# Every 4th or 8th chunk of split weights placed 32, 64 or 96 bytes further in its buffer

## The chip, the cores and the metric

The kernel runs on one core of a Trainium2 chip. The metric is device time in microseconds (us) of one execution. TensorE (PE in the profile) multiplies; its weight loads have a row of their own (PEld). VectorE is DVE, ScalarE is ACT, GpSimd is POOL, and SyncE (SP) starts most transfers. SBUF is the memory on the chip from which all of them read; a buffer's address here means its byte offset within a partition.

## The reference

Two transformer blocks follow each other on one sequence of 256 tokens of width 1024, in float32. Cut to what matters:

```
# first block
proj = rms_norm(x) @ w_in;  x = x + [attention, gated linear attention] @ w_out
h = causal_dwconv(rms_norm(x) @ w_ffn_up)          # 1024 -> 2 x 2816
x = x + (silu(h_gate) * h_val) @ w_ffn_down        # 2816 -> 1024
x = rms_norm(x)
# second block
x = x + 0.5 * g1 * swiglu(h1, ffn1_w_in_2, ffn1_w_out_2)   # 1024 -> 2 x 2816 -> 1024
z = h2 @ w_in_2;  y_a = latent attention @ w_branch_a;  y_b = chunk attention @ w_branch_b
x = x + g2 * ((sigmoid(gate_a) * y_a + sigmoid(gate_b) * y_b) @ w_out_2)
x = x + 0.5 * g3 * swiglu(h3, ffn2_w_in_2, ffn2_w_out_2)
return rms_norm(x)
```

h1, h2 and h3 are normalised x, scaled and shifted by vectors that come from w_ada_2.

## The kernel before

Activations lie feature-major: a tile has 128 features on the partitions and the 256 tokens along the row. A linear layer (`lin_t`) makes 128 output features at a time: it goes over the 128-row blocks k of the weight matrix and adds up in one PSUM bank.

Float32 accuracy is reached with three matmuls for each block. The weights w are split into a rounded part and a rest, w = wh + wl, the activations likewise into xh + xl, and wh·xh, wh·xl and wl·xh are added up. Each of the three loads its own 128x128 weights (a LDWEIGHTS) and streams 256 columns of activations; in the layers that read an unnormalised x it is 258 columns, where the two more carry a shift vector. `lin_r`, used in a few places, swaps the two: activations are the loaded side and 512 columns of weights are streamed.

All weights come from HBM as one stream, packed in the order of their use into 285 chunks of up to 128x1024 (the list `PLAN`, made by `plan`). The class `Stream` handles them: `load` starts a chunk's transfer into a buffer `wraw`; `prep` makes two tiles, `whi` and `wlo`, each from a ring of 4 buffers (`SPLIT_BUFS`), and lets ACT write the rounded part into `whi`; `low` lets DVE write the rest (`wraw` - `whi`) into `wlo`; `next` hands out the blocks of a chunk, normally 8 blocks of 128 columns, so 24 matmuls for a chunk. Eight chunks (`UNCUT`) are not split and are used as plain float32. All instructions are recorded through a helper, so every row of the profile has the line L453; tiles tell them apart: `nh`, `nl` are the halves of a normalised input, `hh`, `hl` those of a feed-forward's hidden layer, `xhi`, `xlo` those of an unnormalised x.

The order in which side work is put between the matmuls is made at build time by a model of the engines' clocks; addresses have no part in it.

In the program before, every `whi` and `wlo` buffer is 4096 bytes long and starts at 64 modulo 128 (for example 78016, 82112, 86208, 90304 for `whi`), and every block of activations that such weights meet starts at 0 modulo 128. A block of weights is 512 bytes of a row, so each load starts at 64 modulo 128 too.

Of the kernel before, what the change touches and what calls it, by code (L numbers as in the profile page):

```python
# [11 lines left out]
F32R = mybir.dt.float32r  # L12
# [6 lines left out]
P = 128  # L19
# [5 lines left out]
CH = 1024  # L25
# [152 lines left out]

LINE = 32
XROW = 9 * LINE  # L180
SKIP = {"const": 0, "y1": 0, "hid1": 0, "ff1": 0, "y2": 0, "att2c": 16, "mgc": 0, "ff2": 0}
RAW_PAIRS = {'w_ffn_up': 2, 'ffn1_w_in_2': 5, 'ffn2_w_in_2': 5}
PLAN, UNCUT = plan()
# [27 lines left out]
class Stream:  # L211
# [20 lines left out]
    def prep(self, upto):  # L232
        while self.n_prep <= min(upto, len(PLAN) - 1):
            c = self.n_prep
            w = CW[c]
            self.load(c)
            raw = self.raw.pop(c)
            self.n_prep += 1
            if c in UNCUT:
                self.ready[c] = (raw, raw)  # L240
                continue
            hi = self.pool.tile([P, CH], F32R, name="whi", bufs=SPLIT_BUFS)
            lo = self.pool.tile([P, CH], F32R, name="wlo", bufs=SPLIT_BUFS)
            self.act.activation(hi[:, :w], raw[:, :w], AF.Copy)
            self.ready[c] = (hi, lo)
            self.owed[c] = (raw, self.clock.t["act"])
# [54 lines left out]
def rows(pool, k, w, name, skip=0, dtype=F32R, **kw):  # L301

    t = pool.tile([P, LINE + k * w if skip else k * w], dtype, name=name, **kw)
    return t[:, skip:skip + k * w].rearrange("p (k w) -> p k w", k=k)


def parts(pool, k, name, skip=0, w=S):

    a, b = (rows(pool, k, w, n, skip) for n in name)
    return Operand(a, b, k)  # L310
# [236 lines left out]
SPLIT_BUFS = 4  # L547
# [3 lines left out]
def block_kernel(ctx: ExitStack, tc: tile.TileContext, xin, wst, adaw, cin, vec, cst_a, cst_b, cst_l, wgu, pos,  # L551
# [161 lines left out]
    def xop():  # L713

        return parts(const, KD, ("xhi", "xlo"), SKIP["const"], XROW)

# [154 lines left out]
    actx = ExitStack()  # L871
    xo = parts(const, KD, ("xhi", "xlo"), SKIP["const"])
    xo.f = rows(ypool, KD, S, "yh", SKIP["y1"], F32)
    ap = actx.enter_context(tc.tile_pool(name="att1", bufs=2))
# [90 lines left out]

    yo = parts(ypool, KD, ("yh", "yl"), SKIP["y1"])
    am = {}
# [167 lines left out]
    for what, n in steps(MIX1):  # L1135
# [23 lines left out]
        else:  # L1159
# [3 lines left out]
            state[what] = True  # L1163
    xo = Operand(None, None, KD, f=rows(const, KD, S, "xg", SKIP["const"], F32, tag="xhi"))
    ss = SumSq("ssa")
# [61 lines left out]
    fp = fctx.enter_context(tc.tile_pool(name="ffn1p", bufs=2))  # L1227
    ho = parts(hpool, NF, ("hh", "hl"), SKIP["hid1"])
    no = parts(hpool, KD, ("nh", "nl"), SKIP["hid1"])
# [607 lines left out]
```

## Time and profile before

| | us |
|---|---|
| median of 3 executions | 886.78 |
| the three executions | 882.56, 886.85, 886.78 |
| the profiled execution | 880.52 |
| its span, first to last instruction | 878.7 |
| PE busy | 865.8 (99%) |
| PEld busy | 835.2 (95%) |
| DVE busy | 699.0 (80%) |
| ACT busy | 501.4 (57%) |

PE is busy when any matmul is under way; since matmuls overlap in the records (each shows 0.28 us, and one starts about every 0.12 us), 99% does not say that they follow each other as closely as they could. Time outside the span is 1.8 us. The granted clock is full (1.00) up to the last microseconds.

### The profile page before, as it was taken

Reading aid. Unit: us, or ns where it says so; the run is one execution under the profiler, and the core shown is the slowest. Engines: PE = TensorE matmul, PEld = TensorE weight load, DVE = VectorE, ACT = ScalarE, POOL = GpSimd, SP = SyncE. Lnnn points to the kernel's source line nnn. Section 1 sums busy time; section 2 is a strip of 40 time slices with the busy share of each in tenths; the row PEclk is TensorE's granted clock in tenths of the full one; section 3 lists DMA queues with packets and bytes.
Section 4 is the critical chain, followed back from the end, with each engine's and each line's share of the span. In section 5 each row is a group of like instructions: output and inputs, shape, how many; then the busy total and the mean of one; then the engine's idle time right before and its main releaser. Section 6 shows DMA issues by size and latency. Waiting matters only on the chain.

```text
span 878.7 us, 18127 instructions
## 1 busy us (share of the span) xinstructions
PE 865.8 (99%) x7290; PEld 835.2 (95%) x7290; DVE 699.0 (80%) x1289; ACT 501.4 (57%) x858; POOL 39.5 (4%) x78
## 2 busy tenths in 40 slices
PE   9999999999999999999999999999999999999996
PEld 7878898999999999999999998999999999999996
DVE  5869677999998889989987789889889985555553
ACT  5846676666665557544554466565646754445441
POOL 0000000000000000010110000000000000000000
PEclk9999999999999999999999999999999999999998
DMA  8534344777777985688898755776777675665541
GB/s 313 185 116 140 120 145 151 261 234 234 229 234 269 305 289 171 234 314 282 313 336 275 258 193 181 258 262 208 232 227 238 193 222 186 189 192 168 192 145 48
DMA packets 54132, 192.05 MB, mean 219 GB/s; under 512 B 6016, under 2 KB 6528, under 8 KB 54048
## 3 DMA queue, kind: packets, MB, share of 16 engines
q1 hardware_dynamic: 42768, 151.28, 51.4%
q0 software_dynamic: 10560, 38.41, 13.7%
q8 instruction: 57, 0.93, 0.4%
q10 hardware_dynamic: 720, 1.21, 0.4%
q14 instruction: 27, 0.22, 0.1%
HBM read 189.82 MB, written 1.05 MB: 217 GB/s over the span
## 4 chain that ended last, share of the span: by engine, by line
PE 95%; DVE 3%; DMA 1%; ACT 1%; issue 0%; DVEq 0%; SPq 0%; ACTq 0%
PE acc L453 89%; PE sca L453 3%; PE sct L453 2%; PE ob L453 1%; DVE wlo L453 1%; DMA wraw<-in_wst_dram 1%; DVE ad L453 0%; DVE x L453 0%; DVE f L453 0%; DVE kf L453 0%; DVE sm L453 0%; DVE kcat L453 0%; DVE m L453 0%; ACT rsqt L453 0%; ACT whi L453 0%
## 5 line engine op out<-in xcount | busy, mean ns | idle before, releaser
L453 DVE TENSOR_TENSOR wlo<-wraw,whi 128x1024 fp32r<-128x1024 f32 (+1 forms) x277 | 333.5, 1211 | 65.8 <-ACT whi L453 65.2
L453 ACT ACTIVATE whi<-wraw 128x1024 fp32r<-128x1024 f32 (+1 forms) x277 | 285.6, 1043 | 47.8 <-issue 30.0
L453 PE MATMUL acc<-nh,whi 128*128 128x256 f32 x1048 | 294.5, 281 | 0.0
L453 PE MATMUL acc<-nl,whi 128*128 128x256 f32 x1048 | 291.9, 279 | 0.0
L453 PE MATMUL acc<-nh,wlo 128*128 128x256 f32 x1048 | 291.5, 278 | 0.0
L453 PEld LDWEIGHTS acc<-nh,whi 128*128 128x128 f32 x1048 | 196.8, 188 | 2.3 <-issue 2.2
L453 PEld LDWEIGHTS acc<-nl,whi 128*128 128x128 f32 x1048 | 196.5, 188 | 0.1
L453 PEld LDWEIGHTS acc<-nh,wlo 128*128 128x128 f32 x1048 | 196.6, 188 | 0.0
L453 PE MATMUL acc<-hh,whi 128*128 128x256 f32 x528 | 147.0, 278 | 0.0
L453 PE MATMUL acc<-hl,whi 128*128 128x256 f32 x528 | 147.0, 278 | 0.0
L453 PE MATMUL acc<-hh,wlo 128*128 128x256 f32 x528 | 146.8, 278 | 0.0
L453 PEld LDWEIGHTS acc<-hh,whi 128*128 128x128 f32 x528 | 99.2, 188 | 0.0
L453 PEld LDWEIGHTS acc<-hh,wlo 128*128 128x128 f32 x528 | 99.0, 188 | 0.0
L453 PEld LDWEIGHTS acc<-hl,whi 128*128 128x128 f32 x528 | 99.0, 187 | 0.0
L453 DVE SCALAR_TENSOR_TENSOR adraw<-adraw,crow 128x1024 f32<-128x1024 f32 x72 | 87.7, 1218 | 6.3 <-DMA adraw<-in_adaw_dram 6.2
L453 PE MATMUL acc<-xhi,whi 128*128 128x258 f32 (+2 forms) x312 | 90.9, 291 | 0.7 <-DVE x L453 0.7
L453 PE MATMUL acc<-xlo,whi 128*128 128x258 f32 (+2 forms) x312 | 87.9, 282 | 0.0
L453 PE MATMUL acc<-xhi,wlo 128*128 128x258 f32 (+2 forms) x312 | 87.6, 281 | 0.0
L453 POOL DMA_DIRECT2D adraw<-in_adaw_dram x72 | 38.1, 529 | 641.5 <-DVE adraw L453 374.7
L453 PEld LDWEIGHTS acc<-xhi,whi 128*128 128x128 f32 (+1 forms) x312 | 58.5, 188 | 3.0 <-issue 2.3
L453 PEld LDWEIGHTS acc<-xlo,whi 128*128 128x128 f32 (+1 forms) x312 | 58.7, 188 | 0.4
L453 PEld LDWEIGHTS acc<-xhi,wlo 128*128 128x128 f32 (+1 forms) x312 | 58.5, 188 | 0.0
(283 smaller groups left out, 1151.2 us busy)
## 6 DMA issues: line engine op xcount, KB each, us to landing
wraw<-in_wst_dram SPq DMA_DIRECT2D x277, 512.0 KB, 4.4
adraw<-in_adaw_dram POOLq DMA_DIRECT2D x72, 512.0 KB, 5.0
wraw<-in_wst_dram SPq DMA_DIRECT2D x7, 256.0 KB, 3.2
rb<-in_rel_dram SPq DMA_DIRECT2D x4, 384.0 KB, 4.4
f<-in_cst_l_dram SPq DMA_DIRECT2D x1, 576.0 KB, 6.4
x<-in_xin_dram SPq DMA_DIRECT2D x2, 256.0 KB, 6.1
x<-in_xin_dram ACTq DMA_DIRECT2D x2, 256.0 KB, 6.6
crow<-in_cin_dram POOLq DMA_DIRECT2D x1, 512.0 KB, 7.6
```

What stands on the lines that cost most here:

```text
L453: return f(*args, **kw)
```

## The change

The buffers `whi` and `wlo` grow by 32 floats (128 bytes), and a chunk's tile is a view of 1024 floats inside. For most chunks the view starts at 0. For a chunk whose number in `PLAN` is divisible by `every` it starts 8, 16 or 24 floats (32, 64 or 96 bytes) in, by a table that gives `every`, the start in `whi` and the start in `wlo` for each matrix.

```
+APART = {"w_ffn_up": (4, 8, 8), "w_ffn_down": (8, 8, 8), "ffn1_w_in_2": (4, 0, 8), "ffn1_w_out_2": (4, 24, 24),
+         "ffn2_w_in_2": (4, 16, 16), "ffn2_w_out_2": (4, 8, 0)}
...
-            hi = self.pool.tile([P, CH], F32R, name="whi", bufs=SPLIT_BUFS)
-            lo = self.pool.tile([P, CH], F32R, name="wlo", bufs=SPLIT_BUFS)
+            every, *apart = APART.get(PLAN[c][0][0], (4, 8, 8))
+            hi, lo = (self.pool.tile([P, CH + LINE], F32R, name=n, bufs=SPLIT_BUFS)[:, a:a + CH]
+                      for n, a in zip(("whi", "wlo"), (0, 0) if c % every else apart))
```

Matrices that the table leaves out have (4, 8, 8). 68 of the 277 split chunks are moved:

| matrix | chunks split | of them moved | whi, wlo by bytes |
|---|---|---|---|
| w_in, w_out | 30 | 8 | 32, 32 |
| w_ffn_up | 40 | 10 | 32, 32 |
| w_ffn_down | 22 | 3 | 32, 32 |
| ffn1_w_in_2 | 44 | 11 | 0, 32 |
| ffn1_w_out_2 | 22 | 6 | 96, 96 |
| w_in_2 to w_out_2 | 53 | 13 | 32, 32 |
| ffn2_w_in_2 | 44 | 11 | 64, 64 |
| ffn2_w_out_2 | 22 | 6 | 32, 0 |

The built program has the same instructions in the same order on every engine, with the same waits. Only addresses differ: the buffers of both rings now lie 4224 bytes apart, those behind them (work tiles, hidden layers) 1024 bytes further up. Modulo 128 nothing moves but the chunks of the table, from 64 to 96, 0 or 32.

## Rows read from the trace of the kernel before

**Rows 1.** The page: busy time by engine, and the chain that ended last.

```profile
PE 865.8 (99%) x7290; PEld 835.2 (95%) x7290; DVE 699.0 (80%) x1289; ACT 501.4 (57%) x858; POOL 39.5 (4%) x78
...
PE 95%; DVE 3%; DMA 1%; ACT 1%; issue 0%; DVEq 0%; SPq 0%; ACTq 0%
PE acc L453 89%; PE sca L453 3%; PE sct L453 2%; PE ob L453 1%; DVE wlo L453 1%; DMA wraw<-in_wst_dram 1%; DVE ad L453 0%; DVE x L453 0%; DVE f L453 0%; DVE kf L453 0%; DVE sm L453 0%; DVE kcat L453 0%; DVE m L453 0%; ACT rsqt L453 0%; ACT whi L453 0%
```

**Rows 2.** The chain in order of time: start, length, work (longest pieces).

```profile
138.44 189.79 PE acc L453 x1566
...
329.09 178.31 PE acc L453 x1560
...
686.37 183.56 PE acc L453 x1554
```

**Rows 3.** Windows in the feed-forwards, 256-column matmuls: first block, ff1, ff2.

```profile
core 0: us, PE busy (x) PEld busy (x) DVE busy (x) ACT busy (x) POOL busy (x), PEclk, DMA share, GB/s
149.50:323.50 174.00, 174.00 (x1477) 173.95 (x1476) 160.26 (x264) 108.40 (x172) 11.10 (x21) 1.00 0.78 252
355.00:506.50 151.50, 151.50 (x1339) 151.50 (x1338) 130.47 (x208) 75.70 (x109) 15.34 (x29) 1.00 0.84 290
711.50:868.00 156.50, 156.50 (x1332) 156.50 (x1331) 87.28 (x110) 73.50 (x104) 0.00 (x0) 1.00 0.54 171
```

**Rows 4.** Timeline of PE at 500 us, in ff1: start and length in us.

```profile
499.74 0.28 PE L453 MATMUL acc<-hh,whi 128*128 128x256 f32 x1
499.86 0.28 PE L453 MATMUL acc<-hl,whi 128*128 128x256 f32 x1
...
500.99 0.28 PE L453 MATMUL acc<-hh,wlo 128*128 128x256 f32 x1
```

**Rows 5.** Timeline of PE at 800 us, in ff2.

```profile
799.79 0.28 PE L453 MATMUL acc<-nh,whi 128*128 128x256 f32 x1
...
801.09 0.28 PE L453 MATMUL acc<-nh,wlo 128*128 128x256 f32 x1
```

**Rows 6.** Windows with no other PE work, outside the feed-forwards.

```profile
115.50:134.00 18.50, 18.50 (x158) 18.45 (x157) 14.15 (x24) 12.44 (x24) 0.00 (x0) 1.00 0.52 172
628.50:653.00 24.50, 24.50 (x213) 24.33 (x212) 20.55 (x37) 11.68 (x18) 1.58 (x3) 1.00 0.79 258
660.00:681.00 21.00, 21.00 (x181) 21.00 (x180) 20.00 (x36) 13.11 (x23) 1.59 (x3) 1.00 0.74 236
```

**Rows 7.** Windows of 258-column matmuls, before ff1's and ff2's stretches.

```profile
330.00:354.00 24.00, 24.00 (x202) 24.00 (x201) 23.62 (x50) 17.50 (x30) 0.53 (x1) 1.00 0.52 177
684.00:710.00 26.00, 26.00 (x217) 25.95 (x216) 24.54 (x47) 18.50 (x29) 0.00 (x0) 1.00 0.59 189
```

**Rows 8.** Timeline of PE where ff1 goes from 258 to 256 columns.

```profile
353.57 0.29 PE L453 MATMUL acc<-xlo,whi 128*128 128x258 f32 x1
353.70 0.28 PE L453 MATMUL acc<-xhi,wlo 128*128 128x258 f32 x1
353.82 0.29 PE L453 MATMUL acc<-xhi,whi 128*128 128x258 f32 x1
...
354.90 0.28 PE L453 MATMUL acc<-nh,whi 128*128 128x256 f32 x1
355.02 0.28 PE L453 MATMUL acc<-nl,whi 128*128 128x256 f32 x1
355.13 0.28 PE L453 MATMUL acc<-nh,wlo 128*128 128x256 f32 x1
```

**Rows 9.** The page's costliest groups: PE's three kinds of inputs, and the split.

```profile
L453 DVE TENSOR_TENSOR wlo<-wraw,whi 128x1024 fp32r<-128x1024 f32 (+1 forms) x277 | 333.5, 1211 | 65.8 <-ACT whi L453 65.2
L453 ACT ACTIVATE whi<-wraw 128x1024 fp32r<-128x1024 f32 (+1 forms) x277 | 285.6, 1043 | 47.8 <-issue 30.0
L453 PE MATMUL acc<-nh,whi 128*128 128x256 f32 x1048 | 294.5, 281 | 0.0
...
L453 PE MATMUL acc<-hh,whi 128*128 128x256 f32 x528 | 147.0, 278 | 0.0
```

## The prediction

> **What bounds the kernel now.** I read the page first: PE is on the chain for 95% of the span, and DVE, the next busiest, for 3% [rows 1]. The chain in order of time then shows that this is no mixture: three pieces of 190, 178 and 184 us, one for each feed-forward, hold nothing but matmuls into `acc` [rows 2], 552 of 879 us. In there no wait can be shortened. What counts is only how soon one matmul follows the other.
>
> That is read from windows laid inside these pieces. In the first block's feed-forward 1477 matmuls stand in 174.0 us, 117.8 ns each; in ff2 1332 in 156.5 us, 117.5 ns; in ff1 1339 in 151.5 us, 113.1 ns [rows 3]. The matmuls are of one shape, and PE is busy for the whole of each window, so PE waits for nobody in any of them. The timeline says the same: 11 steps take 1.25 us at 500 us [rows 4] and 1.30 us at 800 us [rows 5], 113.6 against 118.2 ns. So one and the same program text runs at two paces that lie 4.5 ns apart, about 113.3 (fast) and 117.8 (slow).
>
> What makes the difference? Not the clock, granted in full (1.00) in all three windows. Not transfers: the fast window has the busiest DMA, 0.84 against 0.78 and 0.54. Not DVE or ACT: ff2's window has the least of both per us and is slow. Not the addresses as such, since ff1 and ff2 lay out the same buffers and the weights start at 64 and the activations at 0 modulo 128 in both. And no pace gives way to the other inside a window. It looks like a relation in time between two streams, the load of the next weights and the columns of the running matmul, that is settled when a stretch begins and then repeats itself. In ff1 one sees it settle: the steps of the 258-column matmuls are uneven (0.13 and 0.12 us), and with the third 256-column matmul the steps are down to 0.11 us [rows 8]. Both streams read SBUF, so an address can enter such a relation. That is the lever which this change has; the trace does not show it pulled.
>
> The executions fit this. Against the profiled 880.52 the median is 6.3 us longer, and 1339 matmuls of ff1 at 4.5 ns more are 6.0 us. So I take it, as an estimate, that the usual execution is slow in ff1 too.
>
> **The change part by part.** *Instructions:* none is added, removed or moved, and no wait changes. So nothing new queues behind anything, on any engine or queue, SP's and POOL's included.
>
> *The split on ACT and DVE:* 277 activations of 1043 ns and as many subtractions of 1211 ns [rows 9] write as many bytes as before. I cost it at nothing. The cover is room on DVE: 160 of 174 us in the tightest window [rows 3]. A tenth more on 68 moved chunks would be 68 x 0.12 = 8 us of DVE spread over the kernel, against 14 us idle in that one window, so it would still be hidden.
>
> *The moved chunks themselves:* the trace has no weights at 96, 0 or 32 modulo 128, so the pace in them is bounded. From below by the fast pace, the lowest of any 256-column row. From above by the least regular rows I have, the 258-column matmuls: 24.0 us for 202 and 26.0 us for 217, 118.8 to 119.8 ns on the mean [rows 7], with single steps of 0.13 us [rows 8]. I take 117.8, the slow pace, which lies between and is nearest to these means. Where the stretch was slow before, that costs nothing. In ff1, fast in the profiled execution, 208 matmuls read a moved operand (64 in the way in, where 8 of the moved chunks meet 256 columns and only `wlo` moves; 6 x 24 in the way out), and they lose 208 x 4.5 ns = 0.9 us.
>
> *The chunks after a moved one:* here is the whole gain or loss. Entering and leaving a moved chunk changes the relation between the two streams in mid-run, every 96 matmuls (every 192 in `w_ffn_down`). The relation may settle anew each time, in the slow pace or in the fast one; without the change it never gets a second chance. Bounds for this: all unmoved chunks slow, ff1 included (+6.0 us on the profiled execution), and all of them fast. For the second: of the 1477 matmuls of the first feed-forward's window 13 x 24 = 312 read a moved operand, 1165 do not, and 1165 x 4.5 ns = 5.2 us. In ff2's window 288 do (8 chunks of 24, and 6 chunks in which only `whi` moves, 16 each), 1044 do not: 4.7 us. The stretches outside, 158 + 213 + 181 = 552 matmuls [rows 6] at 116 to 117 ns with windows' edges counted in, keep three quarters unmoved: 414 x 4.5 = 1.9 us. In attention, short matmuls break the stream every few microseconds; there I count nothing.
>
> I take the upper bound for the unmoved chunks: a relation that has its neighbour 4.5 ns away and gets a kick of 32, 64 or 96 bytes some 60 times has many chances to fall into the better one, and the better one, once there, held for 1339 matmuls [rows 3].
>
> *Sum:* 880.5 - 5.2 - 4.7 - 1.9 + 0.9 = 869.6, so 870 us. Every term is an absolute pace, so this end does not depend on which of its executions the kernel before was caught in; against the median of 886.8 it is 1.9% less.
>
> The Trainium skill speaks against all of it. In "SBUF — State Buffer", section "Who interferes with whom", TensorE has two read ports in SBUF, one for the moving operand and one for LDWEIGHTS, independent of each other, and "PE and ACT never wait on anyone". By that no address can change a matmul's pace, and the sum would be the 886.8 of before. The trace agrees only in part: nobody else's traffic moves the pace [rows 3], but something that is not the shape, the clock or another engine does, by 4.5 ns. So I give the rule a rival's chance and not more.
>
> **The rivals.**
>
> *The kick takes in one place only.* If of the two slow feed-forwards only one turns fast, the sum is 880.5 - 5.2 + 0.9 = 876. With ff1 slow and the others fast it is 869.6 + 5.1 = 875. For it: three matrices of different table entries must each fall right. Against it: the same relation, modulo 128, holds in all of them. 874 to 882.
>
> *Nothing happens.* The pace does not hang on the address, or each stretch falls back into the pace it would have had: between 880.5 and 886.8 by the share of fast stretches, and 887 if the usual execution is the slow one throughout. For it: within 174 us of slow pace [rows 3] side work on DVE, ACT and DMA comes and goes and never knocks the relation loose, so it may not be easily moved. 882 to 891.
>
> *Slower: moved chunks run at the pace of the uneven rows, and what follows stays slow.* Some 1310 matmuls read a moved operand (68 chunks of up to 24, less the halves that stay). All of ff1 slow is +6.0 us. At 119.8 ns, the mean of the 258-column row, moved matmuls cost 2.0 ns over the slow pace: 880.5 + 6.0 + 2.6 = 889. At 125 ns, a single step of the uneven kind throughout, they cost 7.2 ns: 880.5 + 6.0 + 9.4 = 896. It decides from 3.6 ns over the slow pace, about 121.4 ns in moved chunks. Against it: no 20 us of this trace run that slowly.
>
> **How the numbers follow.** Kick works in nearly all stretches (862 to 874): 0.44. In one place only (874 to 882): 0.20. Nothing (882 to 891): 0.22. Slower (over 891): 0.14. The lower end: the two feed-forward inputs of the page have 3 x (1048 + 528) = 4728 matmuls [rows 9], with the 552 outside 5280; less the 1339 already fast, 3941 x 4.5 = 17.7 us, and 880.5 - 17.7 = 863 with moved chunks fast as well. The likeliest case alone spans 863 to 874. For 8 in 10 I leave out the slower rival and the top of the third: 863 to 889. Half a per cent is 4.4 us, about what a measurement of this kernel can tell from no change; so faster means under 882.3: 0.44 + 0.20 = 0.64, same 0.22, slower 0.14.
>
> **What would show it.** Right: windows in the first feed-forward and ff2 with about 88 matmuls for each 10 us instead of 85, moved chunks at about 118 ns between chunks at 113; the same counts of instructions; DVE's 1211 ns and ACT's 1043 ns unchanged. Wrong in the step on moved chunks: a pace above 120 ns in every fourth chunk of a timeline. Wrong in the step on what follows: unmoved chunks still at 117.8 in the first feed-forward and ff2, or ff1 fallen to it. Wrong altogether: the two paces as before, in other stretches than before.

## The result and the profile after

The changed kernel takes 873.47 us (median of 4 executions, 873.32 to 873.88), the kernel before 886.75 (882.56 to 886.85): a ratio of 0.985, interval 0.984 to 0.987. The forecast was 870, faster. So the number held; what made it is another matter, as the experiments show. In the comparisons of the experiments the kernel before ran near 881 us about as often as near 887 (17 and 20 of 39 executions), so the gain is 7 to 13 us, by which of the two one meets.

The chain in order of time of the changed kernel, its longest pieces (start, length, work), against [rows 2]:

```profile
138.39 184.33 PE acc L457 x1566
323.58 180.07 PE acc L457 x1560
...
680.57 182.37 PE acc L457 x1554
```

The first block's feed-forward gave 189.79 - 184.33 = 5.5 us, ff2 1.2 us, and ff1, the fast one of before, lost 1.8. The spans differ by 878.7 - 871.8 = 6.9 us, so 2.0 us came from outside the three pieces.

Windows of the changed kernel inside these pieces, then outside them, then in 258-column matmuls, against [rows 3, 6, 7]. A window also counts the two or three matmuls that hang over its edges:

```profile
core 0: us, PE busy (x) PEld busy (x) DVE busy (x) ACT busy (x) POOL busy (x), PEclk, DMA share, GB/s
149.50:318.50 169.00, 169.00 (x1481) 168.95 (x1480) 158.39 (x266) 108.60 (x172) 11.09 (x21) 1.00 0.80 261
349.00:502.00 153.00, 153.00 (x1336) 153.00 (x1335) 131.59 (x208) 76.77 (x110) 15.32 (x29) 1.00 0.83 286
707.00:861.00 154.00, 154.00 (x1321) 154.00 (x1320) 86.02 (x107) 72.24 (x103) 0.00 (x0) 1.00 0.54 171
115.50:134.00 18.50, 18.50 (x160) 18.40 (x159) 13.97 (x24) 12.76 (x24) 0.00 (x0) 1.00 0.51 171
624.50:649.00 24.50, 24.50 (x216) 24.33 (x213) 20.81 (x39) 12.12 (x18) 1.59 (x3) 1.00 0.82 264
655.00:676.00 21.00, 21.00 (x186) 21.00 (x185) 20.46 (x39) 13.57 (x23) 1.67 (x4) 1.00 0.77 251
325.00:348.00 23.00, 23.00 (x194) 23.00 (x193) 22.71 (x48) 16.94 (x27) 0.53 (x1) 1.00 0.55 185
679.00:704.00 25.00, 25.00 (x208) 24.95 (x207) 23.50 (x45) 17.71 (x28) 0.00 (x0) 1.00 0.58 185
```

These are 114.1, 114.5 and 116.6 ns per matmul in the three feed-forwards, means of more than one pace; the granted clock is 1.00 in all windows. Outside, they are 115.6, 113.4 and 112.9 where they were 117.1, 115.0 and 116.0, so most of these stretches turned fast too; the 258-column matmuls stayed at 118.6 and 120.2 where they were at 118.8 and 119.8. The timeline takes the feed-forwards apart: the chunks are counted off in it, 24 matmuls each, back from the first matmul that reads `hh`. In the first block's feed-forward these five rows are the first matmuls of five chunks in a row; the first chunk is a moved one:

```profile
221.21 0.28 PE L457 MATMUL acc<-nh,whi 128*128 128x256 f32 x1
...
224.00 0.28 PE L457 MATMUL acc<-nh,whi 128*128 128x256 f32 x1
...
226.72 0.28 PE L457 MATMUL acc<-nh,whi 128*128 128x256 f32 x1
...
229.44 0.28 PE L457 MATMUL acc<-nh,whi 128*128 128x256 f32 x1
...
232.16 0.28 PE L457 MATMUL acc<-nh,whi 128*128 128x256 f32 x1
```

2.79 us for the moved chunk (about 116.5 ns each), then 2.72 us three times (113.3). The same five places in ff2, again beginning with a moved chunk:

```profile
747.67 0.28 PE L457 MATMUL acc<-nh,whi 128*128 128x256 f32 x1
...
750.54 0.28 PE L457 MATMUL acc<-nh,whi 128*128 128x256 f32 x1
...
753.38 0.28 PE L457 MATMUL acc<-nh,whi 128*128 128x256 f32 x1
...
756.20 0.28 PE L457 MATMUL acc<-nh,whi 128*128 128x256 f32 x1
...
758.92 0.28 PE L457 MATMUL acc<-nh,whi 128*128 128x256 f32 x1
```

2.87 us (about 119.9 ns each) for the moved chunk, 2.84 and 2.82 us (117.9, slow), then 2.72 (113.3, fast). This pattern repeats in every round of four, and in ff2's way out with 117.6 ns in the moved chunk. The important row is the fourth: the time per matmul falls at a chunk that is not moved, behind another that is not moved. In the trace of the kernel before no stretch changes its pace between chunks. Something else than the moved chunks can turn a stretch fast, and the only other thing that the diff changes is that buffers lie 4224 bytes apart instead of 4096. 4224 is 16 times 256 plus 128: modulo 128 all stays as it was, but modulo 256 the unmoved chunks now start at 64 and 192 in turn, where all started at 192 before.

The work on ACT and DVE cost what it did [rows 9]:

```profile
L457 DVE TENSOR_TENSOR wlo<-wraw,whi 128x1024 fp32r<-128x1024 f32 (+1 forms) x277 | 333.5, 1211 | 65.3 <-ACT whi L457 64.4
L457 ACT ACTIVATE whi<-wraw 128x1024 fp32r<-128x1024 f32 (+1 forms) x277 | 285.7, 1044 | 44.6 <-issue 30.3
```

### The profile page after: what moved, and what is told of

Same layout as the page of the kernel before. It is cut to its first block, busy times and chain, and to the rows that moved or that the text cites. A ratio compares the mean times of both kernels' runs of the same rounds, so it can differ in the third digit from the quotient of the medians.

```text
span 871.8 us, 18127 instructions
## 1 busy us (share of the span) xinstructions
PE 857.0 (98%) x7290; PEld 827.0 (95%) x7290; DVE 698.3 (80%) x1289; ACT 502.2 (58%) x858; POOL 39.4 (5%) x78
## 4 chain that ended last, share of the span: by engine, by line
PE 95%; DVE 3%; DMA 1%; ACT 0%; issue 0%; SPq 0%; DVEq 0%; ACTq 0%
PE acc L457 89%; PE sca L457 3%; PE sct L457 2%; DMA wraw<-in_wst_dram 1%; PE ob L457 1%; DVE wlo L457 1%; DVE ad L457 0%; DVE x L457 0%; DVE kf L457 0%; DVE f L457 0%; DVE sm L457 0%; DVE kcat L457 0%; ACT rsqt L457 0%; SPq L457 0%; DVE am L457 0%
## 5 line engine op out<-in xcount | busy, mean ns | idle before, releaser
L457 DVE TENSOR_TENSOR wlo<-wraw,whi 128x1024 fp32r<-128x1024 f32 (+1 forms) x277 | 333.5, 1211 | 65.3 <-ACT whi L457 64.4
L457 ACT ACTIVATE whi<-wraw 128x1024 fp32r<-128x1024 f32 (+1 forms) x277 | 285.7, 1044 | 44.6 <-issue 30.3
```

What stands on the lines that cost most here:

```text
L457: return f(*args, **kw)
```

## The experiments

All kernels have the same instructions in the same order with the same waits; they differ only in where `whi` and `wlo` lie. What lies behind these buffers moves by multiples of 256 bytes, so no run moves an activation modulo 256. Where a cut of code shows added lines alone, they stand in place of the three lines of the change. Theory A is the prediction's: the moved chunks kick the stretches into the fast pace. Theory B: the spacing does it. Each comparison with the kernel before is with its executions on the same chip in the same batch; their medians were 886.5 in the first two batches and 882.8 in the third, all between 880.6 and 887.2.

### The spacing alone, and the moved chunks alone

`e1_pitch_only` keeps the spacing and moves nothing:

```
-                      for n, a in zip(("whi", "wlo"), (0, 0) if c % every else apart))
+                      for n, a in zip(("whi", "wlo"), (0, 0)))
```

> Both rings 4224 bytes apart as in the change, but no chunk moved inside its buffer. Theory A (the moved chunks are what turns the stretches fast, as predicted): nothing is moved, so the two paces stand as in the kernel before, long stretches at 117.8 ns, 880 to 887 us. Theory B (the new spacing of the buffers does it: in the changed kernel's ff2 the pace falls from 117.8 to 113.4 ns at the same buffer in every round of four, with no moved chunk there): stretches turn fast at that buffer and stay fast, and without the moved chunks' own 117 to 120 ns the time is 863 to 868 us, below the changed kernel's 873.5.

Measured: 866.28 us (865.65 to 866.41), ratio 0.979 (0.975 to 0.983). Theory B's number. Windows of this run in the three feed-forwards:

```profile
160.00:315.00 155.00, 154.41 (x1362) 154.22 (x1361) 144.16 (x243) 98.80 (x156) 11.07 (x21) 1.00 0.79 264
360.00:500.00 140.00, 140.00 (x1238) 140.00 (x1237) 119.56 (x189) 70.28 (x102) 15.21 (x29) 1.00 0.86 294
710.00:855.00 145.00, 145.00 (x1282) 145.00 (x1281) 81.67 (x101) 69.26 (x98) 0.00 (x0) 1.00 0.56 172
```

113.8, 113.1 and 113.1 ns: all three fast. In ff1 one can watch a stretch turn. Three first matmuls of chunks, 24 apart, the first chunk at 192 and the second at 64 modulo 256:

```profile
354.79 0.28 PE L457 MATMUL acc<-nh,whi 128*128 128x256 f32 x1
...
357.61 0.28 PE L457 MATMUL acc<-nh,whi 128*128 128x256 f32 x1
...
360.33 0.28 PE L457 MATMUL acc<-nh,whi 128*128 128x256 f32 x1
```

2.82 us, then 2.72 us, and from there fast to the end of ff1. Earlier steps between buffers had passed without effect in this stretch, so one step does not always do it; but there is one in every chunk.

`e2_shift_only` does the reverse. The chunk numbers divisible by 4 always fall on the same buffer of the ring of four, so that buffer gets 256 bytes more and the others none: every unmoved chunk is at 192 modulo 256 as before, and the table's chunks are moved as in the change.

```
+            a, b = (0, 0) if c % every else apart
+            if c % 4:
+                hi, lo = (self.pool.tile([P, CH], F32R, name=n, bufs=3) for n in ("whi", "wlo"))
+            else:
+                hi, lo = (self.pool.tile([P, CH + 2 * LINE], F32R, name=n, tag=n + "0", bufs=1)[:, o:o + CH]
+                          for n, o in (("whi", a), ("wlo", b)))
```

> The chunks of the table moved as in the change, but all buffers placed so that unmoved chunks start at 192 modulo 256, as in the kernel before. Theory A: the first block's feed-forward and ff1 as in the changed kernel, unmoved chunks at 113.3 ns, 871 to 876 us. Theory B: unmoved chunks at 117.8 ns nearly everywhere, moved ones at 116.7 to 119.7, 883 to 889 us.

Measured: 884.43 us (10 executions, 879.95 to 886.60), ratio 0.999 (0.996 to 1.002). Nothing gained, as theory B has it. Windows in the first block's feed-forward, ff1's way in, its way out, ff2's way in, its way out:

```profile
160.00:320.00 160.00, 160.00 (x1360) 160.00 (x1360) 146.02 (x242) 97.58 (x156) 10.82 (x21) 1.00 0.79 257
365.00:430.00 65.00, 65.00 (x554) 65.00 (x554) 58.16 (x97) 32.52 (x50) 7.39 (x14) 1.00 0.84 291
455.00:510.00 55.00, 55.00 (x469) 55.00 (x468) 42.10 (x62) 25.05 (x34) 4.22 (x8) 1.00 0.77 262
725.00:805.00 80.00, 80.00 (x698) 80.00 (x697) 47.48 (x62) 39.07 (x58) 0.00 (x0) 1.00 0.63 194
815.00:870.00 55.00, 55.00 (x469) 55.00 (x468) 28.52 (x33) 24.29 (x32) 0.00 (x0) 1.00 0.41 135
```

117.6, 117.3, 117.3, 114.6 and 117.3 ns. Four entries of the table turned no stretch fast: 32 bytes in both, 32 in `wlo` alone, 96 in both, 32 in `whi` alone. Two of them even ended a fast stretch. ff1 began fast and went slow, for good, at the first chunk in which `wlo` is moved, the second of these three (first matmuls of chunks):

```profile
357.86 0.28 PE L461 MATMUL acc<-nh,whi 128*128 128x256 f32 x1
...
360.58 0.28 PE L461 MATMUL acc<-nh,whi 128*128 128x256 f32 x1
...
363.40 0.28 PE L461 MATMUL acc<-nh,whi 128*128 128x256 f32 x1
```

2.72 us, then 2.82. ff2's way out did the same at the first chunk in which `whi` is moved, from 113.5 to 117.7 ns. The fifth entry, 64 bytes in both, is an exception: in ff2's way in, unmoved chunks ran at 113.3 ns and moved ones at 120.0. But that stretch was fast from its first 256-column chunk (113.4 ns), right behind a moved one of 258 columns, so this run shows that such kicks leave a fast stretch fast and not that they turn a slow one.

### Does a kick of 64 bytes work by itself?

`e7_kick64` has the buffers of `e2_shift_only` and moves every fourth chunk of every matrix by 64 bytes in both:

```
+                hi, lo = (self.pool.tile([P, CH + 2 * LINE], F32R, name=n, tag=n + "0", bufs=1)[:, 16:16 + CH]
+                          for n in ("whi", "wlo"))
```

> Buffers as in the kernel before (192 modulo 256), every fourth chunk of every matrix 64 bytes in, in both buffers: the kick alone, with the size that left ff2's way in fast in the run with the shift alone. Theory A with the right size (64 bytes kick, 32 and 96 do not): unmoved chunks at 113.3 ns in all feed-forwards, moved ones at 119.7: 872 to 876 us. Theory B (ff2 was fast there by its start and only kept it): stretches by chance, moved chunks slower, 882 to 890 us.

Measured: 874.90 us (873.83 to 875.83), ratio 0.989 (0.986 to 0.993). Windows in the three feed-forwards, each a mean of 113.3 ns in unmoved and 120.0 ns in moved chunks:

```profile
160.00:315.00 155.00, 155.00 (x1350) 155.00 (x1349) 143.51 (x239) 96.64 (x154) 10.55 (x20) 1.00 0.79 260
360.00:500.00 140.00, 140.00 (x1221) 140.00 (x1220) 118.86 (x188) 70.15 (x101) 14.78 (x28) 1.00 0.85 293
710.00:855.00 145.00, 145.00 (x1264) 145.00 (x1263) 84.94 (x105) 71.14 (x101) 0.00 (x0) 1.00 0.56 182
```

In the first feed-forward one sees the kick turn a slow stretch. First matmuls of four chunks, the second of them the first moved one:

```profile
152.75 0.28 PE L459 MATMUL acc<-nh,whi 128*128 128x256 f32 x1
...
155.57 0.28 PE L459 MATMUL acc<-nh,whi 128*128 128x256 f32 x1
...
158.45 0.28 PE L459 MATMUL acc<-nh,whi 128*128 128x256 f32 x1
...
161.17 0.28 PE L459 MATMUL acc<-nh,whi 128*128 128x256 f32 x1
```

2.82 us (slow), 2.88 (moved), then 2.72 (fast). ff1 and ff2 were fast in this execution from their first 256-column chunk (113.4 ns) and stayed so; that a stretch at 117.8 ns would have turned there is argued from the four executions, which lie within 2 us, and not shown. So the mechanism of theory A exists. Of the sizes tried at the old spacing only 64 bytes did it, and every moved chunk pays for it. The table uses that size in one matrix of the changed kernel, ff2's way in, and together with the new spacing it comes out badly there: fast before each moved chunk, slow for two chunks behind it. `e4_ff2_like_first` gives ff2 the first block's entries:

```
-         "ffn2_w_in_2": (4, 16, 16), "ffn2_w_out_2": (4, 8, 0)}
+         "ffn2_w_in_2": (4, 8, 8), "ffn2_w_out_2": (8, 8, 8)}
```

> The table's entries for ffn2_w_in_2 and ffn2_w_out_2 replaced by those of the first block, (4, 8, 8) and (8, 8, 8), so 32 bytes in both buffers. In the changed kernel ff2 runs moved, slow, slow, fast (119.7, 117.8, 117.9, 113.5 ns by chunk), the first block 116.7, 113.3, 113.3, 113.3. Both theories: ff2 then runs as the first block does, which over 1300 matmuls is about 3 ns each: 869 to 870 us. If ff2 stays slow, the difference lies in the stage and not in the entry.

Measured: 870.05 us (869.40 to 871.25), ratio 0.984 (0.979 to 0.988). The chain's piece of ff2 went from 182.37 to 178.48 us, so it was the entry and not the stage:

```profile
680.33 178.48 PE acc L457 x1554
```

`e3_all_moved` takes the change away from the kick while keeping the moved address: every chunk is 32 bytes in:

```
-                      for n, a in zip(("whi", "wlo"), (0, 0) if c % every else apart))
+                      for n, a in zip(("whi", "wlo"), (8, 8)))
```

> Every split chunk 32 bytes in, spacing 4224: no change of address modulo 128 ever happens. Theory A: no chunk differs from the next, so there is nothing that kicks; all matmuls run at the pace that moved chunks have in the changed kernel, 116.7 ns, which is 1.1 ns under the slow pace for some 5400 matmuls: 880 to 882 us. Theory B alone (spacing turns any start fast): 863 to 868 us.

Measured: 883.7 us (one execution), some 2 us above theory A's number. Its window in the first feed-forward holds 117.0 ns per matmul, in the other two 116.9 and 116.8:

```profile
160.00:320.00 160.00, 160.00 (x1368) 160.00 (x1368) 146.40 (x245) 98.37 (x157) 11.09 (x21) 1.00 0.78 255
```

By the timeline the chunks take 116.6 and 117.5 ns in turn (weights at 224 and 96 modulo 256), neither of the two paces of before, and no stretch turned fast, although the buffers are spaced as in the change. So the spacing's gain is shown for weights at 64 modulo 128 alone. Nor does the start fix the pace: the same 32 bytes gave 116.5 ns between the changed kernel's fast chunks and 117.8 between the 117.8 ns chunks of `e2_shift_only`.

### Which property of the spacing?

Two readings were left: B1, the start must change by 128 bytes from chunk to chunk; B2, 64 modulo 256 is simply the better place. `e5_all_at_64` puts every buffer at 64 modulo 256, 4096 bytes apart:

```
+            if not self.ready_pad:
+                self.ready_pad.append(self.pool.tile([P, LINE], F32, name="pad1", bufs=1))
+            hi = self.pool.tile([P, CH], F32R, name="whi", bufs=SPLIT_BUFS)
+            lo = self.pool.tile([P, CH], F32R, name="wlo", bufs=SPLIT_BUFS)
...
```

> Buffers 4096 bytes apart as in the kernel before, nothing moved inside them, but all of them 128 bytes further up: every chunk starts at 64 modulo 256 instead of 192. Theory B1 (what helps is that the place changes by 128 bytes from chunk to chunk): no change from chunk to chunk, so stretches at either pace by chance as before, 880 to 887 us. Theory B2 (64 modulo 256 is simply the better place, half the buffers have it under the new spacing): fast nearly everywhere, 863 to 867 us.

Measured: 876.01 us (868.19, 874.51, 877.51, 879.97), ratio 0.990 (0.983 to 0.996): neither number. The profiled execution, the slowest, looks like the kernel before: first feed-forward and ff2 slow (117.6 ns), ff1 fast.

```profile
155.00:320.00 165.00, 165.00 (x1403) 165.00 (x1403) 150.94 (x251) 100.97 (x163) 10.54 (x20) 1.00 0.78 255
...
715.00:865.00 150.00, 150.00 (x1276) 150.00 (x1275) 83.49 (x104) 70.97 (x100) 0.00 (x0) 1.00 0.55 171
```

So the place alone does not make a stretch fast (against B2), and a slow stretch stays slow when no chunk differs from the next (for B1). But the executions scatter over 12 us and lie lower than those of before, the shortest, 868.19, as low as with a step; B1 does not say that. A slow start may be less likely there; only the longest execution was profiled. That is open.

`e6_one_of_four_128` is built like `e2_shift_only`: three buffers of each ring at 192 modulo 256, and in the fourth every chunk 128 bytes further, in `whi` and `wlo` alike:

```
+            if c % 4:
+                hi, lo = (self.pool.tile([P, CH], F32R, name=n, bufs=3) for n in ("whi", "wlo"))
+            else:
+                hi, lo = (self.pool.tile([P, CH + 2 * LINE], F32R, name=n, tag=n + "0", bufs=1)[:, LINE:LINE + CH]
+                          for n in ("whi", "wlo"))
```

> Buffers 4096 bytes apart (192 modulo 256), but every fourth chunk 128 bytes further in both buffers, so at 64 modulo 256. Theory B1: one step of 128 bytes and back in each round of four is enough, stretches turn fast within a few chunks and stay, 865 to 869 us. Theory B2: only the fourth chunk is fast and the rest goes by chance, 878 to 886 us. Against the changed kernel: a moved chunk keeps its address modulo 128, so it should not pay the 116.7 to 119.7 ns.

Measured: 868.78 us (867.46 to 869.68), ratio 0.982 (0.978 to 0.986), B1's number. A window over the first feed-forward has 113.1 ns, moved chunks included, so a step of 128 bytes costs a chunk nothing there:

```profile
160.00:315.00 155.00, 155.00 (x1370) 155.00 (x1369) 145.10 (x243) 99.45 (x156) 11.08 (x21) 1.00 0.81 265
```

The turn does not come at every step: in ff2 the first seven 256-column chunks ran at 117.7 to 118.0 ns, a moved one among them, and the second moved one at 113.4, as did all behind it. In the feed-forwards of the four profiled runs whose weights start at 64 or 192 modulo 256 alone (this one, `e1_pitch_only`, `e8_whi_pitch` and `e9_wlo_pitch`), every turn to the fast pace falls in a chunk at 64 behind one at 192, and none in one at 192 behind one at 64. Why the direction should matter, no run shows.

`e11_whi_step256` asks whether any step does. It spaces `whi` by 4352 bytes, so all stay at 192 modulo 256:

```
+            hi = self.pool.tile([P, CH + 2 * LINE], F32R, name="whi", bufs=SPLIT_BUFS)[:, :CH]
+            lo = self.pool.tile([P, CH], F32R, name="wlo", bufs=SPLIT_BUFS)
```

> whi buffers 4352 bytes apart, so that the place changes by 256 bytes from chunk to chunk, and all stay at 192 modulo 256; wlo as before. If what counts is that the address modulo 256 changes: nothing gained, stretches by chance, 880 to 887 us. If any change of spacing away from 4096 bytes does it: 865 to 869 us.

Measured: 886.64 us (10 executions, 881.02 to 887.24), ratio 1.002 (0.999 to 1.005). Nothing gained. Of the two spacings tried, the one that changes the address modulo 256 helps and the one that keeps it does not.

`e8_whi_pitch` and `e9_wlo_pitch` space only one of the two rings by 4224 bytes, the first `whi`, the second `wlo`:

```
+            hi = self.pool.tile([P, CH + LINE], F32R, name="whi", bufs=SPLIT_BUFS)[:, :CH]
+            lo = self.pool.tile([P, CH], F32R, name="wlo", bufs=SPLIT_BUFS)
```

```
+            hi = self.pool.tile([P, CH], F32R, name="whi", bufs=SPLIT_BUFS)
+            lo = self.pool.tile([P, CH + LINE], F32R, name="wlo", bufs=SPLIT_BUFS)[:, :CH]
```

> Only the whi buffers 4224 bytes apart, wlo 4096 apart and at 192 modulo 256, nothing moved. Two of three matmuls load from whi. If any step of 128 bytes in a stream of loads is enough: 865 to 869 us. If both buffers must step together: stretches by chance or a pace of its own, 875 to 887 us.

> The counterpart of the run with whi alone: only the wlo buffers 4224 bytes apart, whi 4096 apart and at 192 modulo 256. One of three matmuls loads from wlo. If any change of 128 bytes in the stream of loads is enough, 865 to 869 us, as with whi alone (865.4). If whi's step does the work (two loads in a row from one block), stretches by chance, 878 to 887 us.

Measured: `whi` alone 865.35 us (865.28, 865.32, 865.38, 869.53), ratio 0.980 (0.975 to 0.985), the shortest median here, though not to be told from `e1_pitch_only` (0.979, on another chip). `wlo` alone 880.81 us (10 executions, 873.49 to 884.59), ratio 0.996 (0.993 to 0.9995). Windows of the first, in the three feed-forwards, and one of the second, in the first feed-forward:

```profile
160.00:315.00 155.00, 155.00 (x1369) 155.00 (x1368) 144.91 (x244) 99.29 (x155) 11.08 (x21) 1.00 0.81 265
360.00:500.00 140.00, 140.00 (x1238) 140.00 (x1237) 120.35 (x189) 70.91 (x101) 14.79 (x28) 1.00 0.86 296
710.00:855.00 145.00, 145.00 (x1279) 144.66 (x1277) 80.92 (x102) 69.09 (x97) 0.00 (x0) 1.00 0.56 171
```

```profile
160.00:320.00 160.00, 160.00 (x1354) 160.00 (x1354) 145.69 (x239) 96.70 (x155) 10.55 (x20) 1.00 0.78 255
```

113.2, 113.1 and 113.4 ns against 118.2. With `wlo` alone the chunks of the first feed-forward and of ff2 take 117.8 and 118.9 ns in turn, slow to the end. But ff1 turned fast, at the first 256-column chunk with `wlo` at 64 modulo 256, the second of these:

```profile
356.06 0.28 PE L456 MATMUL acc<-nh,whi 128*128 128x256 f32 x1
...
358.89 0.28 PE L456 MATMUL acc<-nh,whi 128*128 128x256 f32 x1
...
361.62 0.28 PE L456 MATMUL acc<-nh,whi 128*128 128x256 f32 x1
```

2.83 us, then 2.73, and fast to the end of ff1. Two of the ten executions, 873.49 and 874.77 us, lie below all of the kernel before. So a step in `wlo` alone can end the slow pace but mostly does not, and the step in `whi` does it in all three feed-forwards. That this is because two of three loads come from `whi` is not shown.

### The kernel before once more

> The kernel before once more, for a second profile. The estimate that its executions differ by which long stretches start fast: an execution near 886.8 us has ff1 at 117.8 ns (151.5 us for 1286 instead of 1339 matmuls), one near 881 us has one long stretch fast; no stretch changes its pace in the middle. If the difference of 6 us lies elsewhere (start, waits, attention), ff1 is fast in both.

Measured: 881.19 us; again ff1 fast and the other two slow, so this execution could not decide it. An execution with all three at 117.8 ns was caught in `e11_whi_step256` instead, whose weights lie as those of before do modulo 256: it took 886.42 us, and its chain shows

```profile
138.37 189.79 PE acc L456 x1566
...
329.03 184.28 PE acc L456 x1560
...
692.28 183.56 PE acc L456 x1554
```

First piece and last as in [rows 2] to 0.01 us, the middle one 184.28 - 178.31 = 6.0 us longer. That is the prediction's estimate of what separates 880.5 from 886.8. It is shown for this kernel; for the kernel before it stays inferred.

## Why the prediction was right in its number and wrong in its cause

**What bounds the kernel: right.** Two paces 4.5 ns apart, settled by something that is neither shape, clock, transfers nor another engine, and that the weights' addresses can move. With only addresses changed, kernels ran from 865.3 to 886.6 us.

**Instructions, ACT and DVE at no cost: right.** 1211 and 1044 ns, DVE's 158 of 169 us still covered.

**The pace in moved chunks, taken as 117.8 ns within 113.3 to 119.8: right on the mean.** In the changed kernel's timeline it is 116.5 for 32 bytes in both, 117.6 to 117.7 for 32 in one, 118.2 for 96, 119.9 for 64. ff1 lost 1.8 us instead of 0.9, for the most part because where only `wlo` is moved I counted the third of the matmuls that read it, and the whole chunk of 24 slowed, and the chunk behind it in part (114.0).

**"Entering and leaving a moved chunk changes the relation between the two streams in mid-run": the step that failed.** That it then settles in the fast pace was taken for all of the table's sizes. With these sizes and the old spacing no feed-forward of the profiled execution turned from slow to fast, two stretches turned from fast to slow, and the time is that of before (`e2_shift_only`, 884.4). Without any moved chunk the gain is larger than with them (`e1_pitch_only`, 866.3 against 873.5). A kick of 64 bytes works (`e7_kick64`), but the table has it in one matrix alone. The prediction put the new spacing at nothing, without a reason: it said what lies where modulo 128 and took the rest for unchanged. The moved chunks cost the changed kernel about 7 us of what the spacing gives. Of that the chain's pieces show 182.37 - 177.65 = 4.7 us in ff2 and 180.07 - 178.50 = 1.6 in ff1, against the run with `whi`'s spacing alone.

**The terms.** That the number came out near is luck. The first feed-forward gave 5.5 us where 5.2 were forecast, since the spacing turns fast just what the kick was to turn. What lies outside the three pieces gave 2.0 where 1.9 were forecast, but only 1.1 of that in the windows of [rows 6]; one of these stood at 115.0 ns before, not at 116 to 117, and had less to give. ff2 gave 1.2 instead of 4.7: its two table entries undo two chunks of three. The sum missed by 3.9 us on the profiled execution (869.6 against 873.55), of which ff2 is 3.5. The signs that the prediction named could not tell kick from spacing: 87.6 matmuls for each 10 us in the first feed-forward came as it said.

**The estimate on the executions: half right.** The 6.0 us between 881 and 887 us are a slow ff1, as far as `e11_whi_step256` shows. But the executions near 887 us are about half of them, and not the usual ones.

**The rivals.** "Nothing happens" is what the moved chunks alone do. "In one place only" describes what came fairly, with the first block turned and ff2 hardly. Slower did not come.

The Trainium skill's rule that the prediction weighed ("SBUF — State Buffer", section "Who interferes with whom": independent ports for the moving operand and LDWEIGHTS, and "PE and ACT never wait on anyone") does not cover this. Nobody else need be waited for, but 128 bytes more between `whi`'s buffers took 2.0% off the time (0.980, 0.975 to 0.985). The measurement decides: where the loaded weights start, from one chunk to the next, matters to a matmul's pace. That it does so by a relation to the stream of activations stays the prediction's reading; no run moved the activations, and where inside the chip the two would meet, no run shows.

## What to carry to other kernels

When equal matmuls run at two paces in different stretches, look at where the loaded operand's buffers start, modulo 256 and not only modulo 128, and try a ring whose spacing changes that from one buffer to the next. Price everything that a diff does to addresses: a buffer that grows to make room for an offset moves all of its neighbours, and here that side effect was the gain, and the offset a cost. When a change works, take its parts one at a time; the part that it is named after may be the one to leave out.

## What the runs showed of the hardware that was not expected

- A stretch of 1300 equal matmuls keeps one of two paces, 113.3 or 117.8 ns, through all that ACT, DVE and DMA do meanwhile, and weights that start 128 bytes further modulo 256 than those before can end the slow one for the rest of the stretch, as in ff1 of `e1_pitch_only`. A pause can bring it back: in ff1 of `e6_one_of_four_128` PE sat idle for 0.39 us at 433 us, and chunks that had run at 113.3 ns ran at 117.8 and 117.7 until the next moved one.
- The paces by the weights' start modulo 128, activations at 0: 64 gives 113.3 or 117.8 ns, 96 gave 116.5 to 117.8 by what stood before, 32 about 118.2, and 0 about 120.0.
- A step of 256 bytes between `whi`'s buffers does nothing (886.64 us), one of 128 gives 865.35 us.
- The kernel before scatters between 880.5 and 887.2 us, and the kernels whose buffers turn every stretch scatter by 2.2 us at most, but for one execution of 869.53 with `whi` alone.
